# The prompt's attention scores as three products on two 64-row halves of the TensorE array

## The chip, the cores and the metric

The kernel runs on one core of a Trainium2 chip. The metric is the device time of one execution in microseconds (us); the time before is the median of three runs. A difference of about 0.2% is what a measurement of this kernel can resolve.

The engines are named as in the profile: PE is TensorE's matrix products, PEld its weight loads (the operand that stays in the array), DVE is VectorE, ACT is ScalarE, POOL is GpSimd, SP is the queue that issues the DMAs. "sc", "tr", "ot" and "mm" are the names of the banks of PSUM, in which PE leaves its results.

## The reference

Two streams of tokens, a prompt of 2048 and a sample of 512, go through two layers of width 1024. Each layer normalises its input, projects it to six groups of columns, pools one half of the channels over windows, runs attention with 4 heads on the other half, gates both, maps them back with one output matrix and adds the normalised result to the input. The part that the change touches is the attention, here cut to its core:

```python
def diff_attention(q, k, v, lam, subln_g, lambda_init):
    ...
    scale = dh ** -0.5                      # dh = 64, two maps per head
    def block(qblk):
        s = jnp.einsum('bqhcd,bkhcd->bhcqk', qblk, k,
                       preferred_element_type=jnp.float32) * scale
        p = jax.nn.softmax(s, axis=-1)
        a = p[:, :, 0] - lam * p[:, :, 1]
        return jnp.einsum('bhqk,bkhe->bqhe', a.astype(v.dtype), v)
    ...
```

A head has two maps of scores, each a product over 64 dimensions. Both are exponentiated over all the keys, and their weighted difference multiplies the values.

## The kernel before

**Precision.** Operands of products are split in two parts: "hi", the value rounded to the type float32r, and "lo", the rest (`split`, lines 106 to 114). A product of two such numbers is the sum of hi x hi, hi x lo and lo x hi; the term lo x lo is small.

**Stages of a layer.** First come the projections of the prompt, with the normalisation and the pooled channels beside them. Queries, keys and values go to DRAM, hi and lo apart. Then comes the attention (`attention`, line 393), with the projections of the sample and later the pooled share of the outputs as filling work for PE. The outputs (`phase3`) end the layer. In the profiled execution the prompt's scores run from 633.8 to about 1447 us in the first layer and from about 2232 to 3017 us in the second.

**The attention's steps.** `blocks` (line 566) walks through heads and blocks of 256 queries. A block of the prompt has two query tiles of 128 and two maps, so four sets of scores. A set is 128 queries against 2048 keys, in four chunks of 512 keys. A step of the loop at line 591 takes four chunks: for the prompt one set, for the sample four sets of one chunk. Each chunk has a bank "sc", of which there are four, so a step's scores overwrite the banks of the step before, once those have been exponentiated. The order on each engine is the order in which the code issues the work.

One step does, in this order:

- for each of the four chunks: its scores (`score`, line 434, PE), the exponential of the same chunk of the step before (`expo`, line 455, ACT), and its maximum over the keys (`peak`, line 443, DVE); behind the fourth chunk the maximum of the four, "nm" (line 453), which the exponentials of this step need;
- behind the first chunk's part (`if j == 0`, line 620), four transpositions of finished weights (`turn`, `flip`, lines 596 and 484), called "early"; behind the fourth chunk four more, called "late";
- the products with the values (`values`, line 500) for tiles that were transposed before;
- the split of the transposed tiles into hi and lo (`flip_split`, ACT and DVE);
- the combination of the two maps of a query tile (`combine`, line 468, POOL);
- six small steps of filling products (`fill`), and the value products of the early tiles.

**The scores.** `load_head` (line 398) brings a head's keys into the tiles "ks": for each map two tiles of 1024 keys, with hi on partitions 0 to 63 and lo on partitions 64 to 127, in two DMAs each. `load_q` puts the queries, hi and lo, on both halves of the partitions. A product with the query's hi part on all 128 rows therefore gives hi x hi and hi x lo at once, and a second with its lo part adds lo x hi and lo x lo:

```python
kk = s["b"]["ks"][m][ch // 2][:, ch % 2 * TB : (ch % 2 + 1) * TB]
nc.tensor.matmul(ps, lhsT=q[:, m, 0, ts], rhs=kk, start=True, stop=False)
nc.tensor.matmul(ps, lhsT=q[:, m, 1, ts], rhs=kk, start=False, stop=True)
```

Of the kernel before, what the change touches and what calls it, by code (L numbers as in the profile page):

```python
# [20 lines left out]
P = 128  # L21
# [29 lines left out]
def f32(ap):  # L51
    return ap.bitcast(F32)
# [3 lines left out]
def trunk_kernel(ctx: ExitStack, tc: tile.TileContext, a, outs):  # L56
# [14 lines left out]
    def bank(tag):  # L71
        """the banks of a tag in turn"""
        taken[tag] += 1
        return psum.tile([P, TB], F32, name=f"{tag}{taken[tag] % BANKS[tag]}")
# [31 lines left out]
    def split(hi, lo, src, hi_eng, lo_eng):  # L106
        """hi = src rounded to float32r, lo = src - hi (exact)."""
        if hi_eng is nc.scalar:
            nc.scalar.activation(hi, src, AF.Copy)  # L109
        elif hi_eng is nc.gpsimd:  # L110
            nc.gpsimd.tensor_scalar(hi, src, 1.0, 0.0, op0=ALU.mult, op1=ALU.add)
        else:
            nc.vector.tensor_copy(hi, src)
        lo_eng.tensor_tensor(lo, src, f32(hi), op=ALU.subtract)  # L114
# [31 lines left out]

    def norm_block(l, c, st, tb, ht, xp, hts, early, free=lambda: True, more=None, slow=0):
        """h of 512 tokens, transposed and split, and their rotary tables; yields between
        small steps"""
        src = st["x"] if l == 0 else st["xs"]  # L150
# [77 lines left out]
    def load_w(raw, p, hi_eng, lo_eng, later=None):  # L228
        """half the rows of the weights of 256 projection columns, split"""
        wh = p["w"].tile([P, 4, 256], F32R, name="wh")  # L230
        wl = p["w"].tile([P, 4, 256], F32R, name="wl")
        if later is None:
            split(wh, wl, raw, hi_eng, lo_eng)
        else:
            later.append(lambda: split(wh, wl, raw, hi_eng, lo_eng))
        return wh, wl

    def project(st, tb, kind, pair, w, ht, p, tag, halfway):
        """a pair of projection chunks for a block of tokens; yields between small steps"""
        hh, hl, cs = ht  # L240
# [43 lines left out]
    def evacuate(st, sl, kind, pair, sub, ps, cs, raws, p):  # L284
        """what follows on a projection chunk, a small step at a time"""
        h = 2 * pair + sub
# [35 lines left out]
    def stream(l, jobs, nxt, hts, p, hook, later):  # L322
        """the projections of a layer: each job is a pair of chunks for some blocks; a
        block yields None between small steps and a chunk's tail; True ends a job"""

        def load(j, raw):
            if j == 1:
                return load_w(raw, p, nc.scalar, nc.vector, later)
            if jobs[j][3] == "sc":
                return load_w(raw, p, nc.scalar, nc.vector)  # L330
            return load_w(raw, p, nc.scalar, nc.gpsimd, later)

        first = nxt
        for j, (kind, pair, turns, tag) in enumerate(jobs):
            w, nxt = first if j == AGAIN else nxt, []
            more = j + 1 < len(jobs) and j + 1 != AGAIN
            if more:
                raws = [load_raw(l, jobs[j + 1], half, p) for half in range(2)]
                nxt.append(load(j + 1, raws[0]))
            for n, (st, tb) in enumerate(turns):  # L340
                hook(j, n)
                last = more and n == len(turns) - 1
                yield from project(st, tb, kind, pair, w, hts[st["n"], tb], p, tag, lambda: nxt.append(load(j + 1, raws[1])) if last else None)
            yield True

    def pool_block(c, st, tb, u_p, t_p, tag):
        """the pooled channels of 512 tokens; yields between small steps"""
        S = st["S"]
# [44 lines left out]
    def attention(c, p, po, fill):  # L393
        """software-pipelined: a step fills four banks with scores while the four of the
        step before are exponentiated and finished blocks are multiplied with the values"""
        EH = 2 * TB

        def load_head(st, h):
# [14 lines left out]
            for m in range(2):  # L413
                for c0 in range(0, S, n):
                    t = p["k"].tile([P, EH], F32R, name="ks")
                    for i in range(2):
                        src = st["ks"][h // 2][h % 2, :, :, m, i, c0 : c0 + n].rearrange("x r n -> (x r) n")
                        nc.sync.dma_start(f32(t[i * 64 : i * 64 + 64, :n]), src)
                    ks[m].append(t)
# [14 lines left out]
        def score(s, ch):  # L434
# [5 lines left out]
            nc.tensor.matmul(ps, lhsT=q[:, m, 1, ts], rhs=kk, start=False, stop=True)  # L440
            s["ps"].append(ps)

        def peak(s, ch):
# [40 lines left out]
        def flip(b, unit):  # L484
            """two key tiles of a query block, keys onto the partitions"""
            ps = bank("tr").rearrange("p (j n) -> p j n", j=2)
# [42 lines left out]
        def squares(b, sq, shl):  # L529
            """the sums of the squares, on all partitions"""  # L530
            ps = bank("tr")
            for i in range(2):
                nc.tensor.matmul(ps[:, :QB], lhsT=ones, rhs=shl[:, i], start=i == 0, stop=i == 1)
            return b, sq, ps

        def scales(b, sq, ps):
            """per query and head, the factor of its normalisation"""
            st, h, qb = b["st"], b["h"], b["qb"]
# [27 lines left out]
        def blocks():  # L566
            """the last prompt head in turn with the sample's heads"""
            nq, ns = pr["S"] // QB, sa["S"] // QB
# [22 lines left out]
        while True:  # L591
# [21 lines left out]
            for j in range(4):  # L613
                if j < len(jobs):
                    score(*jobs[j])
                if j < len(pend):
                    expo(*pend[j])
                if j < len(jobs):
                    peak(*jobs[j])
                if j == 0:  # L620
                    early = turn()
# [51 lines left out]
    def load_wout(l, p, wo, ks, raws, pools):  # L673
        """output weights, split"""
        for k in ks:
# [29 lines left out]
    def pooled_outputs(wo, p):  # L705
        """the pooled channels' share of the outputs, a token tile after the other"""
        todo = [(st, t) for st in streams for t in range(st["S"] // P)]
# [19 lines left out]
    def drop(q):  # L727
        """a step of the first of a queue of generators"""
        if q and next(q[0], q) is q:
            q.pop(0)  # L730

    def each(q):
        """a step of all of them"""
        q[:] = [g for g in q if next(g, q) is not q]

    def phase3(l, wo, scaling, pairs, kept, es, nxt):
        """the outputs; what is left of them is returned for the next layer's begin"""
        y_p = es.enter_context(sbuf("y", 6))
# [8 lines left out]
        def load(st, t):  # L747
            """what a token tile needs, and its scales on the diagonals of matrices"""
            s = dict(st=st, t=t, y=y_p.tile([P, D], F32, name="y"))
# [15 lines left out]
        def scale(s):  # L765
            """the heads' outputs times their scales, which are spread over the partitions first"""
            ps = bank("tr")
# [27 lines left out]
        def post_half(s, ns):  # L795
            """for the kernel's last token tiles, half a tile at a time"""
            st, t, y = s["st"], s["t"], s["y"]
# [69 lines left out]
    class Layer:  # L867
        """a layer; its first block is prepared while the layer before still ends"""

# [58 lines left out]
        def run(self, posts, before):  # L928
# [34 lines left out]
            def advance():  # L963
                """a small step of the projections, and now and then one of what goes on beside"""
                t = next(products)
# [39 lines left out]
            def empty():  # L1005
                """take the last chunk of the filling products out of its bank; split weights"""
                while later:
# [16 lines left out]
            def fill(n):  # L1024
                """a few products of the projections of the other stream, then of the outputs"""
                if not raws and not po:
# [25 lines left out]
            def output_weights():  # L1052
                """once the projections are through, their memory goes to the output weights"""
                right.close()
# [10 lines left out]
            def mix_ahead():  # L1065
                """the first heads' outputs that the outputs start with"""
                while slow:
# [41 lines left out]
def lay_w_in(w):  # L1109
    """columns by kind and pair of heads; of q and k the first halves of the rotary  # L1110
    dimensions of a pair, then the second halves; rows by partition"""
    cols = []
# [55 lines left out]
```

## Time and profile before

| | |
|---|---|
| time, median of 3 runs | 3195.07 us (3192.13 to 3199.23) |
| span of the profiled execution, first to last instruction | 3198.0 us; no time of its own is listed beside it |
| scores of the prompt, first and second products | 432.9 and 406.5 us busy, 1024 each |
| transpositions of the weights (line 491) | 328.3 us busy, 2176 |
| products with the values (line 508) | 370.1 and 220.7 us busy, 2176 and 1088 |
| combination of the maps (lines 481 and 482, POOL) | 328.0 and 666.2 us busy, 288 each |
| exponentials (line 466, ACT) | 733.1 us busy, 1088 |
| maxima (line 450, DVE) | 650.4 us busy, 1024 |

A row of a group in the profile reads: line, engine, operation, output<-inputs, shapes, count, then the busy time in us and the mean of one in ns, then the time that the engine was idle just before these instructions and what it waited for. A row of the time line reads: start and duration in us, engine, line, operation. Products are pipelined, so they overlap in such rows: the time from one start to the next is what one of them costs. A row by stretches gives the stretch, its length, the busy time (and count) of each engine, the granted clock of TensorE as a share of full speed, and the DMAs' share and rate.

### The profile page before, as it was taken

To read this page: it belongs to the slowest core of one execution; us is meant where nothing else is said; L and a number is where in the kernel's file an instruction comes from. 1 tells how busy PE (TensorE), PEld (TensorE's weight loads), DVE (VectorE), ACT (ScalarE), POOL (GpSimd) and SP (SyncE) were. 2 spreads that over 40 slices of the span, in tenths; PEclk is the share of its full clock that TensorE was granted. 3 is DMA by queue.
4 is the path that set the end of the run, shared out by engine and by line. 5 is a ranking of instruction groups with operands and counts; after the bars stand their busy time and mean duration, and the time that the engine had idled before them with its cause. 6 is when DMAs were issued, how large, how long until landed. Compare 5 with 4: busy or idle time off the path is not lost. (4 is left out here: it accounts for less than half of the span.)

```text
span 3198.0 us, 48570 instructions
## 1 busy us (share of the span) xinstructions
PE 3088.4 (97%) x16936; PEld 2601.0 (81%) x16936; DVE 2174.8 (68%) x3289; ACT 1751.7 (55%) x3995; POOL 1856.8 (58%) x2058
## 2 busy tenths in 40 slices
PE   8999999999999999998899999999999999999998
PEld 6898888778887888887688888887788878888876
DVE  3354255588888887877834543555888988877767
ACT  3244233377777777773333442333777777777722
POOL 1000122288998888888820001222989888888888
PEclk9999999999999999999999999999999999999999
DMA  5354357643424334436754544577434243353367
GB/s 199 116 158 145 129 159 207 193 133 98 124 63 133 111 105 133 126 100 237 265 183 118 158 137 137 165 202 214 117 90 122 64 139 112 93 154 111 103 216 241
DMA packets 298902, 464.55 MB, mean 145 GB/s; under 512 B 26144, under 2 KB 180768, under 8 KB 298656
## 3 DMA queue, kind: packets, MB, share of 16 engines
q1 hardware_dynamic: 298656, 461.44, 48.2%
q8 instruction: 134, 2.20, 0.3%
q14 instruction: 112, 0.92, 0.1%
HBM read 293.57 MB, written 167.77 MB: 144 GB/s over the span
## 5 line engine op out<-in xcount | busy, mean ns | idle before, releaser
L450 DVE TENSOR_REDUCE mx<-sc 128x1 f32<-128x512 f32 x1024 | 650.4, 684 | 189.1 <-PE sc L440 187.1
L466 ACT ACTIVATE e<-sc,nm 128x512 f32<-128x512 f32 x1088 | 733.1, 694 | 44.0 <-DVE nm L453 40.0
L482 POOL TENSOR_TENSOR e<-e,e 128x1024 f32<-128x1024 f32 (+1 forms) x288 | 666.2, 2313 | 24.0
L277 PE MATMUL sc<-hth,wh 128*128 128x512 f32 x1408 | 556.0, 395 | 0.0
L277 PE MATMUL sc<-htl,wh 128*128 128x512 f32 x1408 | 554.6, 394 | 0.0
L277 PE MATMUL sc<-hth,wl 128*128 128x512 f32 x1408 | 552.8, 393 | 0.0
L109 ACT ACTIVATE ath<-tr 128x512 fp32r<-128x512 f32 x544 | 327.9, 605 | 236.8 <-PE ot L508 193.5
L439 PE MATMUL sc<-ks,q 128*128 128x512 f32 x1024 | 432.9, 423 | 10.4 <-DMA ks<-ks_p 5.3
L440 PE MATMUL sc<-ks,q 128*128 128x512 f32 x1024 | 406.5, 397 | 0.0
L114 DVE TENSOR_TENSOR atl<-tr,ath 128x512 fp32r<-128x512 f32 x544 | 363.6, 682 | 46.5 <-ACT ath L109 46.3
L508 PE MATMUL ot<-ath,v 128*128 128x256 f32 x2176 | 370.1, 292 | 1.9 <-ACT oc L516 1.9
L491 PE MATMUL tr<-ident,e 128*128 128x128 f32 x2176 | 328.3, 275 | 21.7 <-DVE atl L114 21.3
L491 PEld LDWEIGHTS tr<-ident,e 128*128 128x128 f32 x2176 | 268.5, 141 | 97.9 <-DVE atl L114 34.1
L167 POOL TENSOR_TENSOR rs<-ss,mhalf 128x1 f32<-128x1 f32 x40 | 27.0, 676 | 551.9 <-DVE ss L165 551.8
L481 POOL TENSOR_SCALAR e<-e,nco 128x1024 f32<-128x1024 f32 (+1 forms) x288 | 328.0, 1139 | 15.0
L508 PEld LDWEIGHTS ot<-ath,v 128*128 128x128 f32 x2176 | 312.6, 190 | 22.4 <-ACT oc L516 2.7
L277 PEld LDWEIGHTS sc<-hth,wl 128*128 128x128 f32 x1408 | 264.7, 188 | 59.1
L277 PEld LDWEIGHTS sc<-hth,wh 128*128 128x128 f32 x1408 | 264.8, 188 | 58.5 <-POOL wl L114 0.3
L277 PEld LDWEIGHTS sc<-htl,wh 128*128 128x128 f32 x1408 | 264.9, 188 | 57.6 <-DVE htl L114 0.4
L439 PEld LDWEIGHTS sc<-ks,q 128*128 128x128 f32 x1024 | 194.4, 190 | 64.6 <-ACT e L466 30.8
L114 DVE TENSOR_TENSOR wl<-wr,wh 128x1024 fp32r<-128x1024 f32 x94 | 120.8, 1287 | 182.2 <-ACT wh L109 182.1
L466 ACT ACTIVATION_READ_ACCUMULATOR e<-sc,nm 128x1 f32 x1088 | 231.1, 212 | 0.0
(149 smaller groups left out, 5987.6 us busy)
## 6 DMA issues: line engine op xcount, KB each, us to landing
wr<-in_w_in SPq DMA_DIRECT2D x128, 512.0 KB, 4.2
q<-qs_p SPq DMA_DIRECT2D x128, 256.0 KB, 4.2
ks_p<-hl SPq DMA_DIRECT2D x64, 256.0 KB, 3.5
vs_p<-hl SPq DMA_DIRECT2D x128, 128.0 KB, 2.7
qs_p<-hl SPq DMA_DIRECT2D x64, 256.0 KB, 3.5
mp_p<-hl SPq DMA_DIRECT2D x32, 512.0 KB, 3.8
ks<-ks_p SPq DMA_DIRECT2D x64, 256.0 KB, 5.4
v<-vs_p SPq DMA_DIRECT2D x32, 512.0 KB, 5.5
```

The lines of the kernel that those rows point to most:

```text
L109: nc.scalar.activation(hi, src, AF.Copy)
L114: lo_eng.tensor_tensor(lo, src, f32(hi), op=ALU.subtract)
L167: nc.gpsimd.tensor_tensor(rs, ss, mhalf[:, :1], op=ALU.pow)
L277: nc.tensor.matmul(ps, lhsT=w[k // 4][m][:, k % 4, ns], rhs=h[:, k, :], start=k + i == 0, stop=k == KT - 1 and i == 2)
L439: nc.tensor.matmul(ps, lhsT=q[:, m, 0, ts], rhs=kk, start=True, stop=False)
L440: nc.tensor.matmul(ps, lhsT=q[:, m, 1, ts], rhs=kk, start=False, stop=True)
L450: nc.vector.reduce_max(s["mx"][:, ch : ch + 1], s["ps"][ch], axis=AX.X)
L466: nc.scalar.activation(dst, s["ps"][ch], AF.Exp, bias=s["nm"], accum_out=s["b"]["z"][s["qt"]][:, m, ch : ch + 1])
L481: nc.gpsimd.tensor_scalar(x1[:, :n], x1[:, :n], nco, 0.0, op0=ALU.mult, op1=ALU.add)
L482: nc.gpsimd.tensor_tensor(x0[:, :n], x0[:, :n], x1[:, :n], op=ALU.add)
L491: nc.tensor.transpose(ps[:, j, qt * P : (qt + 1) * P], e[kt // 8][:, kt % 8 * P : (kt % 8 + 1) * P], ident)
L508: nc.tensor.matmul(b["ot"][:, :QB], lhsT=b["vs"][v][kt // 8][:, kt % 8, :], rhs=at[:, j, :], start=unit + i == 0, stop=kt == nkt - 1 and i ...
```

## The change

The keys' tiles are laid out anew: partitions 0 to 63 hold the even chunk of a tile, partitions 64 to 127 the odd chunk, and hi and lo follow each other along the free dimension. The scores of two chunks are now made together (`score_pair`): three products for each chunk, hi x hi, hi x lo and lo x hi, on the 64 rows of its half, alternating between the halves. The term lo x lo is no longer computed. The sample's scores stay with `score`. The early transpositions are issued behind the second chunk's part of the step instead of the first's. Text strings that only document the code are removed as well, which is left out here.

```diff
@@ load_head
-                    t = p["k"].tile([P, EH], F32R, name="ks")
-                    for i in range(2):
-                        src = st["ks"][h // 2][h % 2, :, :, m, i, c0 : c0 + n].rearrange("x r n -> (x r) n")
-                        nc.sync.dma_start(f32(t[i * 64 : i * 64 + 64, :n]), src)
+                    t = p["k"].tile([P, 2, TB], F32R, name="ks")
+                    for half in range(2):
+                        c1 = c0 + half * TB
+                        src = st["ks"][h // 2][h % 2, :, :, m, :, c1 : c1 + TB].rearrange("x r i n -> (x r) i n")
+                        nc.sync.dma_start(f32(t[half * 64 : half * 64 + 64]), src)
                     ks[m].append(t)
...
+        def score_pair(s, ch):
+            pss = [bank("sc"), bank("sc")]
+            q, m = s["b"]["q"], s["m"]
+            ts = slice(s["qt"] * P, (s["qt"] + 1) * P)
+            k = s["b"]["ks"][m][ch // 2]
+            for n, (iq, ik) in enumerate(((0, 0), (0, 1), (1, 0))):
+                for half, ps in enumerate(pss):
+                    rows = slice(half * 64, half * 64 + 64)
+                    nc.tensor.matmul(ps, lhsT=q[rows, m, iq, ts], rhs=k[rows, ik, :], start=n == 0, stop=n == 2)
+            s["ps"] += pss
...
             for j in range(4):
-                if j < len(jobs):
+                if j < len(jobs) and jobs[j][0]["nch"] == 1:
                     score(*jobs[j])
+                elif j < len(jobs) and j % 2 == 0:
+                    score_pair(*jobs[j])
                 if j < len(pend):
                     expo(*pend[j])
                 if j < len(jobs):
                     peak(*jobs[j])
-                if j == 0:
+                if j == 1:
                     early = turn()
```

## The prediction

> **What bounds the kernel now.** I read the page first: busy time by engine, then the chain of work that ended last, then the costliest groups.
>
> ```profile
> span 3198.0 us, 48570 instructions
> PE 3088.4 (97%) x16936; PEld 2601.0 (81%) x16936; DVE 2174.8 (68%) x3289; ACT 1751.7 (55%) x3995; POOL 1856.8 (58%) x2058
> PE 20%; POOL 5%; DVE 5%; issue 1%; ACT 1%; DMA 1%; SPq 0%; POOLq 0%; DVEq 0%; ACTq 0%
> L450 DVE TENSOR_REDUCE mx<-sc 128x1 f32<-128x512 f32 x1024 | 650.4, 684 | 189.1 <-PE sc L440 187.1
> L466 ACT ACTIVATE e<-sc,nm 128x512 f32<-128x512 f32 x1088 | 733.1, 694 | 44.0 <-DVE nm L453 40.0
> L439 PE MATMUL sc<-ks,q 128*128 128x512 f32 x1024 | 432.9, 423 | 10.4 <-DMA ks<-ks_p 5.3
> L440 PE MATMUL sc<-ks,q 128*128 128x512 f32 x1024 | 406.5, 397 | 0.0
> ```
>
> TensorE (PE) has work for 97% of the span and leads the chain. The prompt's scores are 2 x 1024 products of 512 columns, 1024 chunks in all: 512 pairs of chunks, and four chunks to a step, so 256 prompt steps. The 1088 exponentials make 272 steps with the sample's 16. A mean over the whole kernel hides the stage that matters, so I took the two attention stages apart, in the view by stretches (PE, PEld, DVE, ACT, POOL busy):
>
> ```profile
> 634.00:1447.00 813.00, 787.95 (x4757) 672.99 (x4756) 675.35 (x1130) 611.39 (x1566) 698.17 (x776) 0.99 0.40 113
> 2232.00:3025.00 793.00, 772.20 (x4697) 661.35 (x4696) 661.60 (x1116) 600.19 (x1540) 688.32 (x768) 0.99 0.39 113
> ```
>
> Here PE is at 97%, at a granted clock of 0.99, but POOL stands at 86% (698.17 of 813), VectorE (DVE) at 83%, ScalarE (ACT) at 75%. A step takes (813 + 793) / 272 = 5.90 us on average. So PE sets the pace, with others 14 to 25% behind: what it gives up can't all come back. The time line shows one step in detail:
>
> ```profile
> 2701.02 0.40 PE L439 MATMUL sc<-ks,q 128*128 128x512 f32 x1
> ...
> 2706.56 0.40 PE L439 MATMUL sc<-ks,q 128*128 128x512 f32 x1
> 2706.80 0.39 PE L440 MATMUL sc<-ks,q 128*128 128x512 f32 x1
> 2707.03 0.60 PE L491 MATMUL tr<-ident,e 128*128 128x128 f32 x4
> ...
> 2707.70 0.40 PE L440 MATMUL sc<-ks,q 128*128 128x512 f32 x1
> ...
> 2707.93 0.40 PE L439 MATMUL sc<-ks,q 128*128 128x512 f32 x1
> 2707.93 0.19 PEld L440 LDWEIGHTS sc<-ks,q 128*128 128x128 f32 x1
> ...
> 2708.17 0.40 PE L440 MATMUL sc<-ks,q 128*128 128x512 f32 x1
> ...
> 2708.40 0.40 PE L439 MATMUL sc<-ks,q 128*128 128x512 f32 x1
> ...
> 2708.63 0.39 PE L440 MATMUL sc<-ks,q 128*128 128x512 f32 x1
> ...
> 2708.86 0.60 PE L491 MATMUL tr<-ident,e 128*128 128x128 f32 x4
> ...
> 2712.52 0.40 PE L439 MATMUL sc<-ks,q 128*128 128x512 f32 x1
> ```
>
> From one step's first score to the next are 5.54 and 5.96 us. A product lasts 0.40 us, yet the next starts (2708.86 - 2707.70) / 5 = 0.232 us later: that slot is its price, not the 0.40. Each product's weight load runs beside the product before it (the load at 2707.93).
>
> **The change part by part.** *The products.* Before, two chunks cost 4 slots, 4 x 0.232 = 0.93 us. Afterwards they are 6 products on 64 rows. No row of this trace has a product on 64 rows, so its price has to be bounded. If the two halves run side by side, the pair costs 3 slots, 0.70 us. If they run one after the other, 6 slots, 1.39 us. In between stand the weight loads, 6 instead of 4. The closest rows are the value products, which are short enough that the loads show:
>
> ```profile
> 905.58 0.64 PE L508 MATMUL ot<-ath,v 128*128 128x256 f32 x4
> ...
> 906.05 0.40 PE L508 MATMUL ot<-atl,v 128*128 128x256 f32 x2
> ...
> 906.29 0.40 PE L439 MATMUL sc<-ks,q 128*128 128x512 f32 x1
> ```
>
> Four of these with a load each take 0.47 us, 0.118 each. Two loads then fit into one slot of 0.232 only just. If a half's product starts 0.118 after the other's, the pair takes 5 x 0.118 + 0.232 = 0.82 us. Side by side thus saves 0.11 to 0.23 us a pair, 0.22 to 0.46 a step, or 56 to 118 us of PE time over 256 steps. I take side by side, since the load at 2707.93 shows that PE already works on two instructions at once, with 0.34 a step as the middle.
>
> The Trainium skill ("TensorE: Matmul & The Clock Gate", section "Measured speedup vs the span model") gives 3.07 times the speed for four tiles of 32 rows. By it, as an estimate, two halves at the same share of the ideal (0.77) would take 0.70 / 0.77 = 0.91 us a pair and save 0.02, about 10 us in all; no row here can show it.
>
> *The wait for banks.* A step's four scores go into the banks of the four that ACT is exponentiating. Before, each chunk waited for its own exponential. Now the second product of a pair waits for the odd chunk's, and behind it on PE queue the pair's other products, the transpositions, the second pair, the value products and the filling ones; DVE (the maxima) and ACT (the split of the transposed tiles) wait for those.
>
> ```profile
> 2705.42 0.69 ACT L466 ACTIVATE e<-sc,nm 128x512 f32<-128x512 f32 x1
> ...
> 2706.08 0.70 ACT L466 ACTIVATE e<-sc,nm 128x512 f32<-128x512 f32 x1
> 2706.18 2.29 DVE L519 SCALAR_TENSOR_TENSOR mt<-oc,sg,g 128x256 f32<-128x256 f32 x1
> ...
> 2707.41 0.71 ACT L466 ACTIVATE e<-sc,nm 128x512 f32<-128x512 f32 x1
> ...
> 2708.39 2.47 DVE L450 TENSOR_REDUCE mx<-sc 128x1 f32<-128x512 f32 x4
> ...
> 2710.89 0.16 DVE L453 TENSOR_REDUCE nm<-mx 128x1 f32<-128x4 f32 x1
> ...
> 2711.14 0.69 ACT L466 ACTIVATE e<-sc,nm 128x512 f32<-128x512 f32 x1 [0.57 <-DVE nm L453]
> ```
>
> The second exponential ends at 2706.78, 0.22 us after this step's first score began: the pair would stall there. The loop that results is: four exponentials 2.70 (2705.42 to 2708.12); a hand-over of 0.09 (2711.05 to 2711.14, which I take for the others too); the last score; 0.16 until its result is out (0.39 - 0.232); 0.09; the maxima that are still to do, 2.47 / 4 = 0.62 each; the maximum of the four, 0.19 (2710.86 to 2711.05); 0.09. Before, one score (0.46) and one maximum close it: 2.70 + 0.09 + 0.46 + 0.16 + 0.09 + 0.62 + 0.19 + 0.09 = 4.40 us, well inside 5.54. Afterwards it is a whole pair (0.70 until its even chunk is through, staggered or not) and two maxima (1.24): 5.26 us. So the step can't fall below 5.26, and of the 0.34 that PE gives up at most 5.54 - 5.26 = 0.28 is earned. Today this wait hardly exists (idle time before the even score's products):
>
> ```profile
>   ACT e L466: 35.5, 86
> ```
>
> 35.5 us in 86 cases; it will be late next in most steps. I take off a third of the 0.28 for steps in which DVE is held up, as by the 2.29 us row at 2706.18, and get 0.18 us a step.
>
> *The moved transpositions.* The early four now follow the first pair instead of the first chunk: the same work, no DMA among it, past no queue but PE's. Their bank is waited for less. Nothing; without cover it would be at most the 0.24 us of one score later in 256 steps, which the stall above already contains.
>
> *The loads of the keys.* Still 64 issues of 256 KB on SP's queue, in pieces of 2 KB where they were 4 KB.
>
> ```profile
> q<-qs_p SPq DMA_DIRECT2D x128, 256.0 KB, 4.2
> ks<-ks_p SPq DMA_DIRECT2D x64, 256.0 KB, 5.4
> ```
>
> The queries come in pieces of 1 KB and land in 4.2 us, sooner than the keys' 5.4. The waits for them (5.3 us by the L439 row) bound the cost: gone, or doubled, 5 us either way. I take 0.
>
> *Sum.* -0.18 x 256 = -46 us. This is from an execution with a span of 3198.0 us; the median of the timed runs is 3195.07, so I carry the difference over: 3149 us. With 0.05 to 0.28 a step the forecast's own range is 3123 to 3182.
>
> **Rivals.** *A switch of the array's division costs time (slower).* Each step now goes from 128 rows to 64 and back twice: 4 switches, between products which today follow without a gap (2706.80, 2707.03). No row prices one. From below it is 0. If the products under way must first come out, it is 0.39 - 0.232 = 0.16 us; if the weight load waits as well (0.19, the row at 2707.93), 0.35. Four cost 0.64 to 1.40 a step. At 0.64 against the middle saving of 0.34, the step grows by 0.30: +77 us, 3272. At 1.40 against the smallest saving, 0.22, it is +302, 3497. The point from which it decides is 0.34 / 4 = 0.085 us a switch. For it: the two forms are never mixed in this trace. Against it: transpositions and products alternate here without loss, and loads already run ahead. The Trainium skill ("TensorEngine Tiling (Array Packing)", section "Key Properties") states that a change of the tiling mode, not of the tile alone, drains TensorE. By that rule this rival holds, and no run here shows it yet.
>
> *The halves don't run side by side* (the change doesn't do what it says): 1.39 instead of 0.93 a pair, +0.46 x 512 = +236 us, 3431. For it: every product of this trace follows the one before by a whole slot; against it: they all need the same 128 rows, so they couldn't do otherwise.
>
> *The loop takes it all.* PE gets faster, but every step waits for exponentials. It needs only 0.28 us more in the loop, and the 2.29 us row shows that DVE can cause that; against it, the 5.54 step has the slack worked out above. 3195, within 6 us.
>
> **How the numbers follow.** Forecast 0.45 (3149), dear switches 0.32 (3272), loop 0.12 (3195), one after the other 0.11 (3431). A difference of 0.2%, 6 us, is about what a measurement of this kernel can tell from none. Faster 0.45; within 0.2% 0.10 of the loop's 0.12; slower 0.45 (0.32 + 0.11, and the loop's other 0.02). The range of 8 in 10: the low end, 3110, stands 13 us under the forecast's best for key loads that vanish and for maxima that no longer wait. The high end, 3340, holds dear switches up to (145 / 256 + 0.34) / 4 = 0.23 us each. Left out are the rival of 3431 (0.11) and switches beyond that (0.08).
>
> **What would show it.** Side by side: the second product of a pair starts at most 0.12 us after the first, and a third of the pair takes about 0.23. Cheap switches: the transpositions start 0.23 us after the last 64-row product; 0.4 or more, with idle time on PE, shows dear ones. The loop: PE's idle time before the pair's products, put down to the exponentials, grows from 35.5 us to some 100, ACT's wait for the step's maximum shrinks or vanishes, and steps lie near 5.3 to 5.4. I would be wrong in the sum if steps came out under 5.26 (the exponentials overlap more than I think), and in the mechanism if a pair took over 0.93 us with its switches.

## The result and the profile after

| | time, median | ratio to before, 95% interval |
|---|---|---|
| before | 3195.5 us | |
| after | 3279.8 us (3277.22 to 3282.22, 4 runs) | 1.0265 (1.0253 to 1.0277) |

The change makes the kernel 84 us slower. The page of the kernel after (line numbers have moved: 453 is `score_pair`, 463 the maxima, 466 the maximum of the four, 479 the exponentials, 504 the transpositions, 521 the value products):

```profile
span 3279.4 us, 50697 instructions
...
PE 3167.2 (97%) x17960; PEld 2521.7 (77%) x17960; DVE 2191.8 (67%) x3289; ACT 1768.6 (54%) x3995; POOL 1849.9 (56%) x2058
...
PE 24%; DVE 4%; POOL 3%; ACT 1%; issue 1%; DMA 0%; SPq 0%; POOLq 0%; DVEq 0%; ACTq 0%
...
L463 DVE TENSOR_REDUCE mx<-sc 128x1 f32<-128x512 f32 x1024 | 657.1, 685 | 261.4 <-PE sc L453 258.9
L479 ACT ACTIVATE e<-sc,nm 128x512 f32<-128x512 f32 x1088 | 732.7, 691 | 41.9 <-DVE nm L466 40.2
...
L453 PE MATMUL sc<-ks,q 64*128 64x512 f32 x3072 | 530.3, 432 | 13.2 <-ACT e L479 9.5
```

PE is still at 97%, and the scores' busy time has fallen from 432.9 + 406.5 to 530.3 us. Whoever stops here would expect a gain. DVE, ACT and POOL are busy for about as long as before, in a longer span. The loader of the weights (PEld) has 1024 loads more and is busy for 79 us less. That by itself is no loss, since loads for the two halves now run at the same time (six in 0.53 us below, where before each took 0.19). What tells of the loss is the idle time ahead of the transpositions and their loads: the causes listed for line 504 add up to 206 us, where those for line 491 before add up to 57.

The time line of one step, PE alone and then the weight loader (PEld), in which a bracket gives the idle time ahead of a row:

```profile
2783.18 0.40 PE L521 MATMUL ot<-atl,v 128*128 128x256 f32 x2
2783.51 0.96 PE L453 MATMUL sc<-ks,q 64*128 64x512 f32 x6
2784.40 0.66 PE L504 MATMUL tr<-ident,e 128*128 128x128 f32 x4
2784.98 0.96 PE L453 MATMUL sc<-ks,q 64*128 64x512 f32 x6
2785.88 0.66 PE L504 MATMUL tr<-ident,e 128*128 128x128 f32 x4
...
2789.28 0.96 PE L453 MATMUL sc<-ks,q 64*128 64x512 f32 x6
```

```profile
2783.50 0.53 PEld L453 LDWEIGHTS sc<-ks,q 64*128 64x128 f32 x6
2784.40 0.42 PEld L504 LDWEIGHTS tr<-ident,e 128*128 128x128 f32 x4 [0.36 <-issue]
2784.98 0.53 PEld L453 LDWEIGHTS sc<-ks,q 64*128 64x128 f32 x6 [0.17 <-issue]
2785.87 0.42 PEld L504 LDWEIGHTS tr<-ident,e 128*128 128x128 f32 x4 [0.36 <-DVE mx L463]
```

Three things are to be seen. First, the halves do run side by side: six products take 0.96 us and one lasts 0.39, so the last starts 0.57 us after the first; one after the other they would start over 5 x 0.232 = 1.16 us. Second, the loader stops for 0.36 us when PE goes from 64 rows to 128, and for 0.17 on the way to 64. Before, a load ran beside each product; here the first load of a new kind starts only after the slot of the last old product is over, and the first product then waits for that load. Third, the step takes 5.77 us (2783.51 to 2789.28) where it took 5.54. Since two pairs save 0.46, four switches have cost 0.69, 0.17 each.

Over all 256 steps, by the starts of their first scores in the two traces: the step at the first fifth of the list, which nothing but PE holds up, goes from 5.54 to 5.77 us. 0.23 x 256 = 59 us. The other 25 of the 84 us lie in longer steps: over all distances the steps add up to 84 us more than before.

### The profile page after: what moved, and what is told of

Read it like the earlier page. It is cut to its first block, busy times and chain, and to the rows that moved or that the text cites. A ratio compares the mean times of both kernels' runs of the same rounds, so it can differ in the third digit from the quotient of the medians.

```text
span 3279.4 us, 50697 instructions
## 1 busy us (share of the span) xinstructions
PE 3167.2 (97%) x17960; PEld 2521.7 (77%) x17960; DVE 2191.8 (67%) x3289; ACT 1768.6 (54%) x3995; POOL 1849.9 (56%) x2058
## 5 line engine op out<-in xcount | busy, mean ns | idle before, releaser
L463 DVE TENSOR_REDUCE mx<-sc 128x1 f32<-128x512 f32 x1024 | 657.1, 685 | 261.4 <-PE sc L453 258.9
L495 POOL TENSOR_TENSOR e<-e,e 128x1024 f32<-128x1024 f32 (+1 forms) x288 | 659.3, 2289 | 24.0
L453 PE MATMUL sc<-ks,q 64*128 64x512 f32 x3072 | 530.3, 432 | 13.2 <-ACT e L479 9.5
L504 PEld LDWEIGHTS tr<-ident,e 128*128 128x128 f32 x2176 | 236.2, 143 | 195.9 <-DVE mx L463 81.8
L453 PEld LDWEIGHTS sc<-ks,q 64*128 64x128 f32 x3072 | 272.9, 186 | 132.5 <-ACT e L479 36.4
L504 PE MATMUL tr<-ident,e 128*128 128x128 f32 x2176 | 358.6, 290 | 14.2 <-DVE atl L114 13.9
L797 PE MATMUL sc<-woh,hl 128*128 128x512 f32 x640 | 214.1, 410 | 17.7 <-DVE hl L114 13.7
```

What stands on the lines that cost most here:

```text
L453: nc.tensor.matmul(ps, lhsT=q[rows, m, iq, ts], rhs=k[rows, ik, :], start=n == 0, stop=n == 2)
L463: nc.vector.reduce_max(s["mx"][:, ch : ch + 1], s["ps"][ch], axis=AX.X)
L495: nc.gpsimd.tensor_tensor(x0[:, :n], x0[:, :n], x1[:, :n], op=ALU.add)
L504: nc.tensor.transpose(ps[:, j, qt * P : (qt + 1) * P], e[kt // 8][:, kt % 8 * P : (kt % 8 + 1) * P], ident)
L797: nc.tensor.matmul(ps, lhsT=lhsT, rhs=w[:, ns], start=i == 0, stop=i == len(todo) - 1)
```

## The experiments

Two theories went into the runs. **S**: a switch between 128 and 64 rows costs about 0.17 us, a pass there and back 0.34, four switches a step. **L**: the loop of exponentials, pair, two maxima and the exponentials of the next step sets the pace. "Step" below is the first fifth of the 254 distances between steps, as above. All ratios are to the kernel before in the same set of runs.

**Switches alone.** The kernel before, the second product of a prompt chunk on 64 rows:

```diff
-            nc.tensor.matmul(ps, lhsT=q[:, m, 1, ts], rhs=kk, start=False, stop=True)
+            if s["nch"] == 1:
+                nc.tensor.matmul(ps, lhsT=q[:, m, 1, ts], rhs=kk, start=False, stop=True)
+            else:
+                nc.tensor.matmul(ps, lhsT=q[:64, m, 1, ts], rhs=kk[:64], start=False, stop=True)
```

> The kernel before, with the prompt's second product of a chunk on the first 64 rows alone (it leaves out lo x lo): the same number of products, slots and weight loads, but a switch to 64 rows and back for each chunk, eight switches in a step. Theory S: 4 x 0.34 = 1.37 us more in each of 256 steps, about +350 us, 3545 us. Theory L and any theory in which the switch is free: the order, the waits and the maxima are those of before, 3195 us.

Measured: 3515.0 us, 1.0999 (1.0982 to 1.1015). The step grows to 7.02 us, (7.02 - 5.54) / 8 = 0.185 a switch. The number of products and slots is that of before; the chunks look like this on PE:

```profile
2754.34 0.50 PE L443 MATMUL sc<-ks,q 64*128 64x512 f32 x1
...
2754.78 0.50 PE L439 MATMUL sc<-ks,q 128*128 128x512 f32 x1
```

0.44 us from start to start, where it was 0.232 (a first product of a kind is listed from the start of its own load, so such a distance holds that load too). The whole run costs 318 us instead of the 350 expected: the median step grows by 1.48 us, 379 us over 256 steps, and steps that wait for other engines anyway hide part of that; how much was not taken apart.

**The same products with half the switches.** The kernel before in the order of pairs: two products on 128 rows, then two on the same 64.

```diff
+        def score_pair(s, ch):
+            ...
+            for rows, i in ((slice(0, P), 0), (slice(0, 64), 1)):
+                for half, ps in enumerate(pss):
+                    nc.tensor.matmul(ps, lhsT=q[rows, m, i, ts], rhs=k[rows, half * TB : (half + 1) * TB], start=i == 0, stop=i == 1)
```

> The kernel before in the order of pairs, four products for two chunks: two on 128 rows, then two on the first 64 rows, which need the same rows and can't run side by side (lo x lo is left out). As many products on 64 rows as in the run with eight switches a step, but four switches. Theory S, with that run's price of 318 / (8 x 256) = 0.155 us a switch: 4 x 0.155 x 256 = 159 us over the 3198 of the pairs' order, 3357 us. Rival (products on 64 rows are dear in themselves): as in that run, 3515 us.

Measured: 3363.6 us, 1.0524 (1.0507 to 1.0542), step 6.23: (6.23 - 5.56) / 4 = 0.17 a switch, against the 5.56 of the same order without switches (next run). A step of that length, from one first score to the next, and the loader at its first two switches (PE's row merges the two products on 128 rows with the two on 64):

```profile
2776.03 1.29 PE L450 MATMUL sc<-ks,q 128*128 128x512 f32 x4
...
2782.26 1.29 PE L450 MATMUL sc<-ks,q 128*128 128x512 f32 x4
```

```profile
2776.59 0.29 PEld L450 LDWEIGHTS sc<-ks,q 64*128 64x128 f32 x2 [0.36 <-issue]
2777.25 0.42 PEld L501 LDWEIGHTS tr<-ident,e 128*128 128x128 f32 x4 [0.36 <-PE sc L450]
```

The price goes with the number of switches, not with the number of products on 64 rows, which is four a step in both of these runs. S holds.

**The order of pairs alone.** As above, but all four products on 128 rows, and with the early transpositions behind the second chunk.

> The kernel before, with its four products of 128 rows for two chunks issued as in after: both banks at once, the products of the two chunks alternating, the early transpositions behind the second chunk. No product on 64 rows, so no switch. Theory S: as before, 3195 us within 10. Theory L: the order alone makes the second chunk's exponential and two maxima part of the loop, 2.70 + 0.09 + 0.93 + 0.16 + 0.09 + 0.62 + 0.62 + 0.19 + 0.09 = 5.5 us beside the 5.54 that PE needs, and so most of what the change lost: +40 to +85 us, 3235 to 3280 us.

Measured: 3198.3 us, 1.0012 (0.9998 to 1.0026), step 5.56. Neither issuing two chunks at once nor the moved transpositions cost anything that can be measured. L, as the main cause, falls.

**Two switches instead of four.** The kernel after with both pairs next to each other:

```diff
+            early = turn()
             for j in range(4):
                 ...
-                if j == 1:
-                    early = turn()
```

> The kernel after, with the early transpositions moved ahead of the scores, so that a step's two pairs stand next to each other: two switches of the array's division in a step instead of four, everything else as after. Theory S (a pass from 128 rows to 64 and back costs about 0.34 us, 0.20 going in and 0.15 going out, by the starts of the products in the trace of after): 0.34 x 256 = 87 us less than after, 3193 us. Theory L (the loop of exponentials, pair, two maxima sets the step): the second pair now follows the first at once and still needs the fourth exponential, so nothing is gained, 3280 us or more.

Measured: 3264.1 us, 1.0218 (1.0202 to 1.0233). This miss is instructive. The step at the first fifth fell to 5.44, the 0.34 that S had asked for; but only a third of the steps are that short, and the median is 5.85. The time line of PE, PEld, ACT and DVE around the pairs:

```profile
2782.26 0.69 ACT L479 ACTIVATE e<-sc,nm 128x512 f32<-128x512 f32 x1
...
2783.93 2.12 PE L453 MATMUL sc<-ks,q 64*128 64x512 f32 x12
...
2784.24 0.71 ACT L479 ACTIVATE e<-sc,nm 128x512 f32<-128x512 f32 x1
...
2784.91 2.48 DVE L463 TENSOR_REDUCE mx<-sc 128x1 f32<-128x512 f32 x4 [1.21 <-PE sc L453]
...
2785.09 0.53 PEld L453 LDWEIGHTS sc<-ks,q 64*128 64x128 f32 x5 [0.41 <-ACT e L479]
...
2787.43 0.16 DVE L466 TENSOR_REDUCE nm<-mx 128x1 f32<-128x4 f32 x1
...
2787.68 0.69 ACT L479 ACTIVATE e<-sc,nm 128x512 f32<-128x512 f32 x1
```

The second pair stalls for the fourth exponential (0.41 us of idle loader), and then four maxima run in a row: from exponential to exponential are 5.42 us, as many as PE needs itself in a step without a stall. So there is no slack left that a delay on DVE or ACT could go into. The idle time agrees. Ahead of the scores, put down to the exponentials (us, then cases), it is

```profile
  ACT e L479: 99.0, 297
```

against 45.9 in 145 in the kernel after. Ahead of the transpositions the wait for the split grew from 38.4 to 77.0 us. Together these are 92 us more, which is of the size of the 71 us that did not come. So L is there, behind S: it takes most of what S gives back.

**Half the maxima.** The kernel after, with the maxima of even chunks alone:

```diff
-            nc.vector.reduce_max(s["mx"][:, ch : ch + 1], s["ps"][ch], axis=AX.X)
+            if ch % 2 == 0:
+                nc.vector.reduce_max(s["mx"][:, ch // 2 : ch // 2 + 1], s["ps"][ch], axis=AX.X)
...
```

> The kernel after, with the maxima of a set taken over its even chunks alone (the odd chunks are left out of the shift of the exponentials): DVE does two maxima a step less, and the loop is shorter by 0.62 us. Theory S: PE's own sum sets the step, 3280 us, at most 15 us less. Theory L: the step falls by what the loop stood above PE's sum, 50 us or more, to 3230 us or less.

Measured: 3242.4 us, 1.0148 (1.0133 to 1.0163), step 5.77 as before the edit. So PE's own sum sets the short steps, as S says, but 37.4 us come out of the long ones, more than S allowed. The control, the same edit on the kernel before:

> The kernel before, with maxima over the even chunks alone (the odd chunks are left out of the shift). It tells whether the 38 us that the same edit took off the kernel after belong to the change. If they are DVE's load in steps where it is held up, which before has as well: 20 to 40 us less here too, 3155 to 3175 us. If they come from the pair's two maxima at once: 3195 us, no gain.

Measured: 3182.3 us, 0.9957 (0.9942 to 0.9972), 13.6 us less. The result lies between the two expectations: part of the 37.4 us is DVE's load in general, and 37.4 - 13.6 = 24 us belong to the change. With half the maxima in both, the two kernels stand 3242.4 - 3182.3 = 60 us apart, which is the 59 us of 256 x 0.23. That splits the 84: 60 for switches less slots saved, 24 that go away with the maxima. To put these 24 down to the loop is an argument, since no run kept the maxima and took the loop alone away.

**Both edits.**

> Both edits on the kernel after: the two pairs of a step next to each other (two switches a step), and maxima over the even chunks alone (the odd chunks are left out of the shift). Theory S with the loop behind it: with pairs together PE's sum is 5.43 us a step, and only the loop over exponentials and four maxima in a row kept the steps at 5.85; with two maxima fewer the loop is 1.24 us shorter and PE sets the step again, 0.34 x 256 = 87 us under the 3242 of the run with even maxima: 3155 us. Rival (two adjacent pairs stall on the hand-over of the banks whatever DVE does): the fourth exponential still ends late, 3225 us or more.

Measured: 3196.4 us, 1.0001 (0.9991 to 1.0010). The step at the first fifth is 5.43, and over half of the steps are under 5.5. The other 40 us that were expected are lost in one step of four, 6.8 us on average in the first three heads, where the other three take 5.43 to 5.50 (the starts of the layers left out). There the sums of squares of a finished block stand in front of the early transpositions. Such a step (2466.93 to 2473.30, 6.37 us) has two waits in the rows of the loader:

```profile
2468.09 0.53 PEld L453 LDWEIGHTS sc<-ks,q 64*128 64x128 f32 x5 [0.40 <-ACT e L480]
...
2472.72 0.42 PEld L505 LDWEIGHTS tr<-ident,e 128*128 128x128 f32 x4 [0.24 <-DVE atl L114]
```

The second pair waited for the fourth exponential, and later the transpositions for their bank ("tr"), until the split on DVE had ended; the next pairs wait behind them on PE's queue. The squares' own products add one slot. Over the run, against the run with even maxima and the pairs apart, idle time put down to the exponentials grew from 37.7 to 72.0 us and that put down to the split from 32.5 to 56.1. So the bank of the transpositions is only the smaller part of it.

**Where the transpositions stand.** Four more runs moved them, with all maxima and with the even ones. Behind both pairs:

> The kernel after, with both pairs of a step first and the eight transpositions behind them: two switches a step, and the early transpositions no longer stand ahead of the pairs, where they waited for the bank that the sums of squares use. Theory S with the loop behind it: PE's sum is 5.43 us as in the run with pairs together; the step with the squares, 6.80 on average there, falls to about 6.1 (6.27 of after less 0.34, with some waits), -0.7 x 64 = -45 us; the four maxima in a row still hold every other step near 5.85: 3264 - 45 = 3220 us. Rival (pairs at the step's beginning stall for the fourth exponential in every step): 3264 us or more.

> The same with maxima over the even chunks alone (the odd chunks are left out of the shift). Theory S with the loop behind it: three steps of four at 5.43 us, as in the run with pairs together and even maxima, and the one with the squares at about 6.1 instead of 6.82: 3196 - 0.7 x 64 = 3150 us, so 30 us less than the kernel before with the same maxima (3182): what the 64-row products earn once two of four switches and the loop are out of the way. Rival (the fourth exponential stalls the pairs): 3196 us or more.

Measured: 3295.6 us, 1.0311 (1.0296 to 1.0326), and 3267.3 us, 1.0224 (1.0207 to 1.0241). Both expectations were wrong and the rival right: idle time ahead of the pairs, put down to the exponentials, is 150.3 us in 403 cases in the first of them, against 45.9 in 145 in the kernel after:

```profile
  ACT e L479: 150.3, 403
```

Without transpositions between or ahead of the pairs PE has less to do until the fourth exponential. The last two runs put them ahead of the pairs, except in the step behind the squares:

```diff
+            early = None if scaling else turn()
             for j in range(4):
                 ...
+            if scaling:
+                early = turn()
```

> Pairs together and maxima over the even chunks alone (the odd chunks are left out of the shift), early transpositions ahead of the pairs except in the step behind a block's sums of squares, where they follow the pairs. In the run with pairs together and even maxima three steps of four took 5.43 us and the fourth, with the squares, 6.82, since the transpositions in front of the pairs waited there for the split on DVE that frees their bank. Theory S with the loop behind it: the fourth falls to about 6.1 (5.43, the squares' 0.24, and the stall of 0.41 for the fourth exponential that the runs with pairs first show): 3196 - 0.7 x 64 = 3150 us. Rival (the fourth step is long for another reason): 3196 us.

> The same with all four maxima, so that the whole result is computed as after. Theory S with the loop behind it: the fourth step falls from 6.80 to about 6.2 against the run with pairs together, the other three stay between 5.43 and 6.07 because of four maxima in a row: 3264 - 0.6 x 64 = 3226 us. Rival: 3264 us.

Measured: 3183.9 us, 0.9966 (0.9955 to 0.9978), and 3238.6 us, 1.0137 (1.0122 to 1.0152). About a quarter and two thirds of the expected gain came. In the first of them the idle time put down to the split fell from 56.1 to 12.0 us, but that put down to the exponentials rose from 72.0 to 80.8, and the step behind now takes 6.0 us on average where it took 5.5. The first run is below both kernels, but it owes that to the maxima: the kernel before with the same maxima takes 3182.3. No order that was tried lets the 64-row products earn anything over the 128-row ones.

**Half by half.** The kernel after with the loops of `score_pair` exchanged, three products of one half ahead of three of the other:

> The kernel after, with a pair's three products of the first half issued before the three of the second. If PE starts products strictly in their order, only the third and the fourth can overlap, five slots instead of three: 2 x 0.232 x 512 = 238 us more than after, 3518 us, a little less where the loop hides it. Rival (PE takes the next product whose half is free): 3280 us.

Measured: 3279.0 us, 1.0260 (1.0239 to 1.0280), the same as after. The six products of a pair still take three slots, so PE does not hold a product back because an earlier one of the other half is still waiting:

```profile
2782.96 0.97 PE L453 MATMUL sc<-ks,q 64*128 64x512 f32 x6
```

## Why the prediction was wrong

- **The bound** was right: PE sets the step, and a slot is 0.232 us. With half the maxima the short steps stay at 5.77 us.
- **The products** were right as far as they went. Side by side, six in three slots; the saving is the upper end of the bounds (0.46 a step), since the two halves, their loads too, start together (3 ns apart) and not 0.118. The twofold speed is also more than the share of 3.07 in 4 from the Trainium skill ("TensorE: Matmul & The Clock Gate", section "Measured speedup vs the span model") would have given.
- **The step that failed** is the sum's silent term: four switches a step were put in at nothing. The rival had the term and nearly its size, "it is 0.39 - 0.232 = 0.16 us; if the weight load waits as well (0.19, the row at 2707.93), 0.35". Measured are 0.17, twice the 0.085 from which that rival was to decide. The mechanism is that of its upper end (the load waits as well), the size that of the lower, because both parts are smaller than it took them. In the step above the first load of the new kind starts 0.32 us after the last product of 512 columns, whose slot is 0.232, and 0.20 after the last transposition, whose slot is 0.11: 0.09 behind the slot both times, not 0.16. And of the load itself only a part is added, as the longest row of a kind, the first behind a switch, shows beside the median one (shortest, median and longest in ns):

```profile
L453 PE MATMUL sc<-ks,q x6: 386/394/497, 2783.5 to 2784.1; 64*128 64x512 f32 x6
```

```profile
L504 PE MATMUL tr<-ident,e x4: 272/273/327, 2784.4 to 2784.8; 128*128 128x128 f32 x4
```

That is 0.10 into a score and 0.05 into a transposition, not 0.19. So the switch to 64 rows costs about 0.19 and the one back 0.14, and the four of a step 0.66, beside the 0.69 worked out from the step. The sign that the prediction set for a wrong mechanism has come: a pair with its two switches takes 0.70 + 0.34 = 1.04 us, over the 0.93. With the 0.46 of the products and 0.69 of the switches the prediction's own sum gives 3195 + 59 = 3254; the rest goes away with half the maxima. That the rival's 3272 us lie only 8 us from the 3279.8 measured is partly luck: its step grows by 0.30 instead of 0.23, and the 25 us of the longer steps are not in it.
- **Why it was ranked second**: "transpositions and products alternate here without loss, and loads already run ahead" was held against it. Both rows are true and neither bears on it: in all of them the array is used as one piece of 128 rows. A trace that never shows a case is no evidence on its cost. The Trainium skill ("TensorEngine Tiling (Array Packing)", section "Key Properties") says that a change of the tiling mode drains TensorE. This case agrees as far as the rows go: the first load of the other mode starts only 0.32 us after the start of the last product of 512 columns (0.89 - 0.57 in the step above), with 0.36 us of idle loader ahead of it. Whether every result is out by then, the rows can't tell, as the 0.39 that they list for a product has a modelled end.
- **The wait for banks and the loop** exist, but as an addition to the switches (24 us, if all that goes away with the maxima is theirs) instead of a cap on a gain. The idle time ahead of the scores that was to grow from 35.5 us to some 100 is 45.9, which fits a longer step that leaves the exponentials more time. Where switches were taken away it did grow: 99.0 us with the pairs together, 150.3 with the pairs first.
- **The moved transpositions** cost nothing (1.0012, 0.9998 to 1.0026, together with the order of pairs). **The loads of the keys** cost nothing either: 5.2 us to landing in pieces of 2 KB, against 5.4 in pieces of 4 KB.

What stays open: the 24 us put down to the loop are a difference of two runs with half the maxima, and how they divide between DVE's held-up steps and the wait for the odd chunk's exponential was not measured. Why the loader waits 0.09 us beyond the slot is not shown either.

## What to carry to other kernels

By the numbers of this case, products on part of the array are worth their slots only in long stretches: with 0.17 us a switch, two switches a stretch and 0.23 us saved a pair, a stretch has to hold at least two pairs before it earns anything. Here a stretch of two pairs was tried in six runs, and waits for the exponentials and the transpositions' bank took what it saved. Before taking a saving on an engine, write down the operations at its edges, where the new kind meets the old, and give each a price from both sides, even when the trace has none. And a change that shortens the engine in front should be summed against the loop behind it: here that stood 0.28 us off by the prediction's sum (5.26 beside 5.54), so that even removing half of the switches brought 16 us instead of 87.

## What the runs showed of the hardware

- Two products on different halves of the rows run side by side at full speed each: six of 512 columns in three slots of 0.232 us, with a weight load for every one (6 loads, 0.53 us in all).
- Their order in the program does not matter within a pair: three of one half ahead of three of the other take the same 0.97 us (3279.0 against 3279.8 us), where a start in strict order would have needed two more slots, 238 us over the kernel by the estimate on record. The Trainium skill ("TensorE: Matmul & The Clock Gate", section "The mechanism") calls products strictly first in, first out; across halves these runs do not agree.
- A switch between 128 and 64 rows costs 0.17 to 0.185 us by three kernels (four, four and eight switches a step), averaged over the two directions, and it shows as idle time of the weight loader. By its parts it is 0.19 into a product of 512 columns and 0.14 into a transposition; six of the eight switches in the dearer kernel lead into such products, against half of them in the other two. The profile's name for what ended the idle time cannot be trusted: in the kernel after it is put down to the maxima (81.8 us) and to "issue" (51.0), and with half of the maxima gone the same gap of 0.36 us is put down to "issue" almost alone:

```profile
PEld tr L505 <- issue: 127.6, 349, 0.6
```
